# When the DeltaNet mixer's products come later in the written order

## The chip, the cores and the metric

The kernel runs as one program on one core of a Trainium2 chip. What is compared is the device time of one execution in microseconds (us), as the median of several runs.

## The reference

The reference is one step of a two-layer decoder trunk over 1,048 tokens: 8 samples that each add one token to an old state, 16 meta tokens and a prompt of 1,024. The first layer mixes tokens with a gated delta rule of 8 heads (128 wide), the second with latent attention; each is followed by a feed-forward layer with a short convolution. The change touches the first layer's mixer alone. Cut to that:

```
proj = h @ w_in                       # q, k, v (8 heads of 128 each), z, a, b
q, k, v = silu(causal convolution of width 4 over q, k, v)
q, k = l2norm(q), l2norm(k);  beta = sigmoid(b);  g = -exp(a_log) * softplus(a + dt_bias)
# prompt, in chunks, for each head; gc = cumulative sum of g inside the chunk
T = unit lower triangular matrix of (beta k k^T) * decay
u, w = solve(T, beta v), solve(T, beta k exp(gc))
for each chunk:                       # the recurrence
    v_new = u - w @ S
    o = (q exp(gc)) @ S + ((q k^T) * decay) @ v_new
    S = S * exp(gc_last) + (k exp(gc_last - gc))^T @ v_new
# samples: one step of the same rule from a state of their own
out = (rmsnorm(o) * silu(z)) @ w_out
```

The states S, the last rows before the convolution and the trunk's result are outputs.

## The kernel before

All matrices lie with channels on the partitions and tokens along the free dimension. TensorE's products with weights are made in three passes (`mm3`): weights and activations are each split into a high and a low part, and high x high, high x low and low x high are summed. The 1,048 tokens are cut into `CH`, pieces of 280, 384 and 384 columns.

The mixer is written as several streams (generators), one for each head and stage, and `merge` interleaves them: each stream yields a position before a piece of work, and the piece with the smallest position is written next. One unit is one head.

- `inproj(h)` runs from h to h + 1: the input projections (`psu`, 24 matmuls a piece) of q, k, v of head h and z of the head before. ScalarE copies a piece out of its bank (line 538, line 533 for the first piece); the projections have two banks (`mtile`).
- `chunks(h)` runs from h + 0.65 to h + 1.9, for 9 chunks of 116 tokens in three groups: transposes of k (`pstr`), the normalised `Kh` and its transposes (`pskt`, line 596), products `pskk` and the decay `E`; a store and reload of `U` in blocks of 32 (`ud`, `ins`); a substitution of 31 steps on VectorE (`tm`, `xs`, lines 658 and 660); a store and reload of the result (`xd`, `X`); products of blocks that complete the inverse (`psr`, line 680, `psx`, `psr2`, `psx2`), and u and w (`psu_`, `psw`), with GpSimd's `KG` and `KL`.
- `recur(h)` runs from h + 1.9 to h + 2.55: nine steps, in three groups. A step has `p1` = w S (line 754), a part of `pso`, `vn` on VectorE (line 757), `p2` (line 759), the rest of `pso` and the new `S` (line 765). After a group come the squares' sums and their scale `f`, the scaled output `on` (line 775), its turn by three transposes (`psot`, line 778), the product with the gate `z` (`og`, line 782) and the store to `og_d`. `on` and `og` take turns in one buffer (tag "on", one buffer). After the groups come the samples: `qkv8` normalised, `ps8t`, the product `p8`, a store of `vn` and its broadcast reload `vr`, the output `o8` and its turn (`pso8`, line 823), and the new states.
- `late_params` loads eight rows of the feed-forward convolution and turns them (`pfr`, line 488), in the buffers of tag "tm", which the substitution uses too.
- At the end `tail_a` and `tail_c` make the output projections of heads 0 to 5 (`psop`), `tail_b` turns the tokens once more (`pxr`, in `psA`); heads 6 and 7 follow.

Three pools hold the mixer's PSUM banks: `psA` has three (tag "g", the products of `chunks`), `psS` two for the recurrence's squares (`p1`, `p2`, `p8`), `psB` one, which `pso`, `psot`, `ps8t` and `pso8` share.

The written order is not yet the order on the engines: the framework that lowers the kernel offers instructions in the written order and places each on its engine when its inputs are there by its own model of the times. Then the order of each engine is fixed, and so is SP's, which issues nearly all transfers. On the chip an engine that comes to an instruction whose inputs are late waits.

Of the kernel before, what the change touches and what calls it, by code (L numbers as in the profile page):

```python
# [11 lines left out]
F32 = mybir.dt.float32  # L12
# [3 lines left out]
ALU = mybir.AluOpType  # L16
AX = mybir.AxisListType
PSUM = bass.MemoryType.PSUM
DRAM = bass.MemoryType.DRAM

P = 128
D = 1024
KT = D // P
NS = 8
# [37 lines left out]
def tile_step(ctx: ExitStack, tc: tile.TileContext, I, O, stop=None):  # L62
# [75 lines left out]
    def vc(nm, k=0):  # L138
        return vec[:, vcol[nm] + k:vcol[nm] + k + 1]
# [221 lines left out]
    psS = es.enter_context(tc.tile_pool(name="gsq", bufs=2, space=PSUM, reuse_waits="tile"))  # L361
    psB = es.enter_context(tc.tile_pool(name="gso", bufs=1, space=PSUM, reuse_waits="tile"))
# [34 lines left out]
    def gates():  # L397
# [65 lines left out]
        ps1 = psS.tile([P, NCK, H], F32, tag="s", name="psgl")  # L463
# [16 lines left out]
    def late_params():  # L480
        for l in range(2):
            for j in range(4):
                yield 2.0 + 0.08 * (4 * l + j)
                frow = rp.tile([2 * NFT, P], F32, tag="tm", name="frow")
                src = I["f_conv_w"][l, j] if j < 3 else I["f_conv_b"][l]
                SP.dma_start(frow, src.rearrange("(t p) -> t p", p=P))
                pt = psA.tile([P, 2 * NFT], F32, tag="g", name="pfr")
                PE.transpose(pt, frow, ident[:2 * NFT, :2 * NFT])
                V.tensor_copy(fcv[:, l, j, :], pt)
# [70 lines left out]
    def chunks(h, p0, p1):  # L560
# [12 lines left out]
        for g in range(3):  # L573
# [19 lines left out]
            yield pos(0.05 + 0.10 * g)  # L593
# [4 lines left out]
            yield pos(0.08 + 0.10 * g)  # L598
# [75 lines left out]
        for g in range(3):  # L674
            yield pos(0.73 + 0.02 * g)
            psr[g] = psA.tile([P, 3, 64], F32, tag="g", name="psr")
            R[g] = rp.tile([P, 3, 64], F32, tag="R", name="R", bufs=3)
            for i in range(3):
                k = 3 * g + i
                PE.matmul(psr[g][32:64, i, 0:32], U[0:32, k, 32:64], Tt[0:32, k, 0:32], start=True, stop=True)  # L680
                PE.matmul(psr[g][96:C, i, 0:32], U[64:96, k, 96:C], Tt[64:96, k, 0:32], start=True, stop=True)
            A.copy(R[g][32:64, :, 0:32], psr[g][32:64, :, 0:32])
            A.copy(R[g][96:C, :, 0:32], psr[g][96:C, :, 0:32])
        for g in range(3):
            gs = slice(3 * g, 3 * g + 3)
            yield pos(0.79 + 0.02 * g)
            psx = psA.tile([P, 3, 64], F32, tag="g", name="psx")
            for i in range(3):
                k = 3 * g + i
                PE.matmul(psx[0:32, i, 0:32], R[g][32:64, i, 0:32], X[32:64, k, 32:64], start=True, stop=True)  # L690
                PE.matmul(psx[64:96, i, 0:C - 96], R[g][96:C, i, 0:32], X[96:C, k, 96:C], start=True, stop=True)
                PE.matmul(psx[32:64, i, 32:64], X[32:64, k, 32:64], R[g][32:64, i, 0:32], start=True, stop=True)
            V.tensor_scalar(X[0:32, gs, 32:64], psx[0:32, :, 0:32], -1.0, None, op0=ALU.mult)
            V.tensor_scalar(X[64:96, gs, 96:C], psx[64:96, :, 0:C - 96], -1.0, None, op0=ALU.mult)
            V.tensor_scalar(Tt[32:64, gs, 0:32], psx[32:64, :, 32:64], -1.0, None, op0=ALU.mult)
# [7 lines left out]
        for g in range(3):  # L703
            yield pos(0.85 + 0.015 * g)
# [5 lines left out]
        for g in range(3):  # L710
            gs = slice(3 * g, 3 * g + 3)
            yield pos(0.9 + 0.015 * g)
# [6 lines left out]
        for g in range(3):  # L719
            gs = slice(3 * g, 3 * g + 3)  # L720
            yield pos(0.95 + 0.015 * g)
# [12 lines left out]
    def recur(h, p0, p1):  # L734
# [6 lines left out]
        S = None  # L741
        Ss = hp.tile([P, NS, P], F32, tag="Ss", name="Ss")
        SP.dma_start(Ss, I["state_delta_S"][0, :, h].rearrange("s k v -> k s v"))
        for g in range(3):
            gs = slice(3 * g, 3 * g + 3)
            pso = psB.tile([P, 3, P], F32, tag="o", name="pso")
            for i in range(3):
                yield pos(0.7 * (3 * g + i) / 9)
                k = 3 * g + i
                if S is None:  # L750
                    vn = uB[:, k, :]
                else:
                    p1_ = psS.tile([P, P], F32, tag="s", name="p1")
# [4 lines left out]
                p2 = psS.tile([P, P], F32, tag="s", name="p2")  # L758
# [17 lines left out]
            ps = psB.tile([P, 3 * C], F32, tag="o", name="psot")  # L776
            for i in range(3):
                PE.transpose(ps[:, C * i:C * i + C], on[:, i, :], ident[:C, :C])
            n = 3 * C if g < 2 else NP - 6 * C
            o0 = NS + 3 * C * g  # L780
            og = rp.tile([P, 3 * P], F32, tag="on", name="og", bufs=1)
            V.scalar_tensor_tensor(og[:, :n], ps[:, :n], vc("a_out"), hd["z"][:, o0:o0 + n], op0=ALU.mult, op1=ALU.mult)
            SP.dma_start(og_d[h][:, o0:o0 + n], og[:, :n])
# [11 lines left out]
        ps = psB.tile([P, 2, NS], F32, tag="o", name="ps8t")  # L795
# [4 lines left out]
        yield pos(0.78)  # L800
        p8 = psS.tile([P, P], F32, tag="s", name="p8")
# [9 lines left out]
        o8 = rp.tile([NS, P], F32, tag="vn", name="o8")  # L811
# [9 lines left out]
        yield pos(0.85)  # L821
        ps = psB.tile([P, NS], F32, tag="o", name="pso8")
        PE.transpose(ps, o8, ident[:NS, :NS])
        og8 = rp.tile([P, NS], F32, tag="og8", name="og8")
        V.scalar_tensor_tensor(og8, ps, vc("a_out"), hd["z"][:, 0:NS], op0=ALU.mult, op1=ALU.mult)
        SP.dma_start(og_d[h][:, 0:NS], og8)
# [5 lines left out]
        SP.dma_start(O["s_delta_S"][0, :, h].rearrange("s k v -> k s v"), Ss)  # L832

# [854 lines left out]
```

## Time and profile before

| | |
|---|---|
| median of 3 runs | 3309.26 us (3307.54 to 3319.37) |
| the profiled execution | 3314.68 us, its span 3312.9 us |
| mean granted TensorE clock | 0.975 |
| TensorE, matmuls | busy 94% of the span |
| VectorE, ScalarE, GpSimd | busy 61%, 38%, 26% |

The span runs from the first to the last instruction of the profiled execution; around it lie 1.8 us of that execution's time. The clock is given as a share of full speed. In the profile PE is TensorE's matmuls, PEld its weight loads, DVE VectorE, ACT ScalarE, POOL GpSimd, SPq the queue of SP; L778 is line 778 of the kernel, and `psot<-ident,on` says that `psot` is written from `ident` and `on`. The squares `p1`, `p2` and `p8` appear as `p`, and `pso8` as `pso`.

### The profile page before, as it was taken

Reading aid. Unit: us, or ns where it says so; the run is one execution under the profiler, and the core shown is the slowest. Engines: PE = TensorE matmul, PEld = TensorE weight load, DVE = VectorE, ACT = ScalarE, POOL = GpSimd, SP = SyncE. Lnnn points to the kernel's source line nnn. Section 1 sums busy time; section 2 is a strip of 40 time slices with the busy share of each in tenths; the row PEclk is TensorE's granted clock in tenths of the full one; section 3 lists DMA queues with packets and bytes.
Section 4 is the critical chain, followed back from the end, with each engine's and each line's share of the span. In section 5 each row is a group of like instructions: output and inputs, shape, how many; then the busy total and the mean of one; then the engine's idle time right before and its main releaser. Section 6 shows DMA issues by size and latency. Waiting matters only on the chain.

```text
span 3312.9 us, 52527 instructions
## 1 busy us (share of the span) xinstructions
PE 3123.5 (94%) x20846; PEld 2884.2 (87%) x20846; DVE 2030.3 (61%) x4139; ACT 1254.9 (38%) x2541; POOL 862.2 (26%) x1013
## 2 busy tenths in 40 slices
PE   7999999999899999999978999999998999999997
PEld 6888888888799999999967888856678999999996
DVE  4777777766864555555576676544557355555556
ACT  4656555563433222222334444433224322222223
POOL 1433222210342222322342111111105332322322
PEclk9999999999899999999989999999998999999999
DMA  3222222235321111111121000354432111111111
GB/s 107 62 65 69 64 67 59 72 105 176 96 66 46 39 52 49 48 46 39 45 86 44 25 27 28 108 189 184 159 102 84 46 46 45 46 45 52 46 39 66
DMA packets 267650, 235.08 MB, mean 71 GB/s; under 512 B 57919, under 2 KB 246597, under 8 KB 263285
## 3 DMA queue, kind: packets, MB, share of 16 engines
q1 hardware_dynamic: 260224, 189.69, 19.7%
q0 software_dynamic: 6912, 41.95, 3.4%
q8 instruction: 164, 2.69, 0.3%
q14 instruction: 82, 0.66, 0.1%
q10 hardware_dynamic: 268, 0.09, 0.0%
HBM read 198.84 MB, written 33.40 MB: 70 GB/s over the span
## 4 chain that ended last, share of the span: by engine, by line
PE 76%; DVE 14%; DMA 3%; issue 3%; ACT 2%; POOL 1%; SPq 0%; ACTq 0%; POOLq 0%; DVEq 0%
PE fps L228 9%; PE fps L229 9%; PE fps L227 9%; PE fdn L228 5%; PE fdn L227 5%; PE fdn L229 5%; PE psu L227 2%; PE psu L229 2%; PE po L1408 2%; PE psu L228 2%; PE dscr L1493 2%; DVE acc L287 2%; PE psop L227 1%; DVE tm L658 1%; DVE xs L660 1%
## 5 line engine op out<-in xcount | busy, mean ns | idle before, releaser
L144 POOL TENSOR_TENSOR ws<-ws,vec 128x1024 f32<-128x1024 f32 (+1 forms) x127 | 249.5, 1965 | 424.3 <-DMA ws<-in_f_w_up_dram 210.1
L228 PE MATMUL fps<-xfl,wh 128*128 128x384 f32 (+1 forms) x1056 | 343.7, 326 | 8.2 <-POOL xfl L295 8.1
L227 PE MATMUL fps<-xfh,wh 128*128 128x384 f32 (+1 forms) x1056 | 341.8, 324 | 8.0 <-ACT xfh L293 7.0
L228 PE MATMUL fps<-xbl,wh 128*128 128x384 f32 (+1 forms) x1056 | 343.6, 325 | 4.8 <-POOL xbl L295 4.7
L227 PE MATMUL fps<-xbh,wh 128*128 128x384 f32 (+1 forms) x1056 | 341.6, 324 | 1.1 <-ACT xbh L293 0.5
L229 PE MATMUL fps<-xfh,wl 128*128 128x384 f32 (+1 forms) x1056 | 342.4, 324 | 0.0
L229 PE MATMUL fps<-xbh,wl 128*128 128x384 f32 (+1 forms) x1056 | 341.2, 323 | 0.0
L966 DVE TENSOR_TENSOR fu<-fps,RS 128x384 f32<-128x384 f32 x176 | 98.0, 557 | 386.6 <-PE fps L229 386.1
L151 ACT CAST wh<-ws 128x1024 fp32r<-128x1024 f32 (+1 forms) x144 | 148.0, 1027 | 491.6 <-PE fps L228 373.8
L227 PE MATMUL fdn<-gh,dh 128*128 128x384 f32 (+1 forms) x960 | 315.2, 328 | 0.0
L228 PE MATMUL fdn<-gl,dh 128*128 128x384 f32 (+1 forms) x960 | 311.6, 325 | 0.0
L229 PE MATMUL fdn<-gh,dl 128*128 128x384 f32 (+1 forms) x960 | 308.6, 321 | 0.0
L1044 DVE TENSOR_TENSOR acc<-acc,fdn 128x384 f32<-128x384 f32 (+1 forms) x432 | 216.7, 514 | 108.8 <-PE fdn L229 108.0
L227 PE MATMUL psu<-xah,wh 128*128 128x384 f32 (+1 forms) x768 | 261.8, 341 | 9.5 <-ACT u L533 5.1
L228 PE MATMUL psu<-xal,wh 128*128 128x384 f32 (+1 forms) x768 | 260.0, 339 | 0.7 <-DVE xal L223 0.7
L229 PE MATMUL psu<-xah,wl 128*128 128x384 f32 (+1 forms) x768 | 259.0, 337 | 0.7 <-DVE wl L152 0.7
L975 DVE SCALAR_TENSOR_TENSOR fy<-fu,fcv,fy 128x1064 f32<-128x1064 f32 x176 | 238.6, 1357 | 7.6 <-ACT fy L973 7.3
L152 DVE TENSOR_TENSOR wl<-ws,wh 128x1024 fp32r<-128x1024 f32 (+1 forms) x144 | 173.6, 1206 | 71.3 <-ACT wh L151 71.1
L228 PEld LDWEIGHTS fps<-xfl,wh 128*128 128x128 f32 x1056 | 200.7, 190 | 10.8 <-POOL xfl L295 10.5
L227 PEld LDWEIGHTS fps<-xfh,wh 128*128 128x128 f32 x1056 | 200.3, 190 | 9.4 <-ACT xfh L293 7.9
L228 PEld LDWEIGHTS fps<-xbl,wh 128*128 128x128 f32 x1056 | 200.5, 190 | 6.9 <-POOL xbl L295 6.5
L227 PEld LDWEIGHTS fps<-xbh,wh 128*128 128x128 f32 x1056 | 200.2, 190 | 1.7 <-ACT xbh L293 0.9
(963 smaller groups left out, 7856.1 us busy)
## 6 DMA issues: line engine op xcount, KB each, us to landing
ws<-in_f_w_up_dram SPq DMA_DIRECT2D x88, 512.0 KB
ds<-in_f_w_down_dram SPq DMA_DIRECT2D x44, 512.0 KB
ws<-in_a_w_in_dram SPq DMA_DIRECT2D x32, 512.0 KB
xt<-in_x_prompt_dram SPq DMA_DIRECT2D x16, 512.0 KB
of<-og_d SPq DMA_DIRECT2D x32, 192.0 KB
xr<-x_d SPq DMA_DIRECT2D x16, 384.0 KB
GC<-gcd SPq DMA_DIRECT2D x24, 174.0 KB
Ss<-in_state_delta_S_dram SPq DMA_DIRECT2D x8, 512.0 KB
```

The lines of the kernel that those rows point to most:

```text
L144: G.tensor_tensor(st, st, bc(fo, [P, kt, m]), op=ALU.mult)
L151: A.copy(hi, st)
L152: V.tensor_tensor(lo, st, hi, op=ALU.subtract)
L227: PE.matmul(ps, wh, ah, start=start, stop=False)
L228: PE.matmul(ps, wh, al, start=False, stop=False)
L229: PE.matmul(ps, wl, ah, start=False, stop=stop)
L287: V.scalar_tensor_tensor(a_[:, k + j, :], a_[:, k + j, :], vc(wname, k + j), res[j], op0=ALU.mult, op1=ALU.add)
L966: V.tensor_tensor(u[:, 18 + t0:18 + t0 + n], ps[:, :n], RS[:, t0:t0 + n], op=ALU.mult)
L975: V.scalar_tensor_tensor(y, u[:, j:j + LW], fcv[:, l, j, tl:tl + 1], y, op0=ALU.mult, op1=ALU.add)
L1044: V.tensor_tensor(acc[c][:, m, :], acc[c][:, m, :], ps[:, :n], op=ALU.add)
L1408: PE.matmul(po[:, :nq], vt[:kk, kb, P * (h % 2):P * (h % 2) + P], pT[:kk, j, :nq], start=(kb == 0), stop=(kb == i))
L1493: PE.matmul(sc[32 * j:32 * j + 32, :], ql[:, k, b, :], cT[:, j, :], start=(k == 0), stop=False, tile_position=(0, 32 * j))
```

## The change

- The turn of a group's outputs (`psot`, `og`, the store) becomes `turn()`. It is called in the third step of the next group, for the last group at position 0.82 of `recur`, ahead of `p8`.
- The squares of the recurrence become four quarters of one tile in one bank (`sq4`); `pso` has two banks for itself, and `psot`, `ps8t`, `pso8` and the gates' `psgl` come from `psA`.
- The second half of a recurrence step has a position of its own, half a step later.
- `pskt` and `pskk` get positions 0.02 later; the block products begin later and follow each other more closely; the last part of `chunks` begins at 0.965 instead of 0.95.
- The samples' product `p8` goes from 0.78 to 0.82, the samples' turn from 0.85 to 1.25, behind the states; `o8` lies in another buffer for it.
- The rows of the feed-forward convolution come at distances of 0.16 instead of 0.08, and each is turned 0.1 after its load.

```diff
     psA = es.enter_context(tc.tile_pool(name="gps", bufs=3, space=PSUM, reuse_waits="tile"))
-    psS = es.enter_context(tc.tile_pool(name="gsq", bufs=2, space=PSUM, reuse_waits="tile"))
-    psB = es.enter_context(tc.tile_pool(name="gso", bufs=1, space=PSUM, reuse_waits="tile"))
+    psS = es.enter_context(tc.tile_pool(name="gsq", bufs=1, space=PSUM, reuse_waits="tile"))
+    psB = es.enter_context(tc.tile_pool(name="gso", bufs=2, space=PSUM, reuse_waits="tile"))
+    sq4 = psS.tile([P, 4, P], F32, name="sq4")
+    nsq = [0]
+
+    def square():
+        nsq[0] += 1
+        return sq4[:, nsq[0] % 4, :]
...
         V.tensor_copy(gc, ps1[:C])
-        ps1 = psS.tile([P, NCK, H], F32, tag="s", name="psgl")
+        ps1 = psA.tile([P, NCK, H], F32, tag="g", name="psgl")
...
             for j in range(4):
-                yield 2.0 + 0.08 * (4 * l + j)
+                yield 2.0 + 0.16 * (4 * l + j)
...
                 SP.dma_start(frow, src.rearrange("(t p) -> t p", p=P))
+                yield 2.1 + 0.16 * (4 * l + j)
...
             V.tensor_tensor(Kh[:, gs, :], ps[:C], bc(rk, [C, 3, P]), op=ALU.mult)
-            yield pos(0.05 + 0.10 * g)
+            yield pos(0.07 + 0.10 * g)
...
             A.copy(kt[:, 32 + 3 * C * g:32 + 3 * C * (g + 1)], ps.rearrange("p a b -> p (a b)"))
-            yield pos(0.08 + 0.10 * g)
+            yield pos(0.10 + 0.10 * g)
...
         for g in range(3):
-            yield pos(0.73 + 0.02 * g)
+            yield pos(0.795 + 0.012 * g)
...
             gs = slice(3 * g, 3 * g + 3)
-            yield pos(0.79 + 0.02 * g)
+            yield pos(0.84 + 0.012 * g)
...
         for g in range(3):
-            yield pos(0.85 + 0.015 * g)
+            yield pos(0.885 + 0.012 * g)
...
             gs = slice(3 * g, 3 * g + 3)
-            yield pos(0.9 + 0.015 * g)
+            yield pos(0.925 + 0.012 * g)
...
             gs = slice(3 * g, 3 * g + 3)
-            yield pos(0.95 + 0.015 * g)
+            yield pos(0.965 + 0.012 * g)
...
         S = None
+        done = []
+
+        def turn():
+            g, on = done.pop()
+            ps = psA.tile([P, 3 * C], F32, tag="g", name="psot")
+            for i in range(3):
+                PE.transpose(ps[:, C * i:C * i + C], on[:, i, :], ident[:C, :C])
+            n = 3 * C if g < 2 else NP - 6 * C
+            o0 = NS + 3 * C * g
+            og = rp.tile([P, 3 * P], F32, tag="on", name="og", bufs=1)
+            V.scalar_tensor_tensor(og[:, :n], ps[:, :n], vc("a_out"), hd["z"][:, o0:o0 + n], op0=ALU.mult, op1=ALU.mult)
+            SP.dma_start(og_d[h][:, o0:o0 + n], og[:, :n])
+
...
                 k = 3 * g + i
+                if i == 2 and done:
+                    turn()
...
                 else:
-                    p1_ = psS.tile([P, P], F32, tag="s", name="p1")
+                    p1_ = square()
...
                     V.scalar_tensor_tensor(vn, p1_[:C, :], nbt[:, k, h:h + 1], uB[:, k, :], op0=ALU.mult, op1=ALU.add)
-                p2 = psS.tile([P, P], F32, tag="s", name="p2")
+                yield pos(0.7 * (3 * g + i + 0.5) / 9)
+                p2 = square()
...
             V.tensor_tensor(on, pso[:C], bc(f, [C, 3, P]), op=ALU.mult)
-            ps = psB.tile([P, 3 * C], F32, tag="o", name="psot")
-            for i in range(3):
-                PE.transpose(ps[:, C * i:C * i + C], on[:, i, :], ident[:C, :C])
-            n = 3 * C if g < 2 else NP - 6 * C
-            o0 = NS + 3 * C * g
-            og = rp.tile([P, 3 * P], F32, tag="on", name="og", bufs=1)
-            V.scalar_tensor_tensor(og[:, :n], ps[:, :n], vc("a_out"), hd["z"][:, o0:o0 + n], op0=ALU.mult, op1=ALU.mult)
-            SP.dma_start(og_d[h][:, o0:o0 + n], og[:, :n])
+            done.append((g, on))
...
         yield pos(0.75)
-        ps = psB.tile([P, 2, NS], F32, tag="o", name="ps8t")
+        ps = psA.tile([P, 2, NS], F32, tag="g", name="ps8t")
...
         V.tensor_copy(kqz[:, 32:32 + 65 * 7 + 1:65], ps[:, 0, :])
-        yield pos(0.78)
-        p8 = psS.tile([P, P], F32, tag="s", name="p8")
+        yield pos(0.82)
+        turn()
+        p8 = square()
...
         SP.dma_start(vr, vd.rearrange("s v -> (s v)").partition_broadcast(P).rearrange("p (s v) -> p s v", s=NS))
-        o8 = rp.tile([NS, P], F32, tag="vn", name="o8")
+        o8 = sq[:, 1, :]
...
         V.tensor_scalar(o8, o8, qk, None, op0=ALU.mult)
-        yield pos(0.85)
-        ps = psB.tile([P, NS], F32, tag="o", name="pso8")
-        PE.transpose(ps, o8, ident[:NS, :NS])
-        og8 = rp.tile([P, NS], F32, tag="og8", name="og8")
-        V.scalar_tensor_tensor(og8, ps, vc("a_out"), hd["z"][:, 0:NS], op0=ALU.mult, op1=ALU.mult)
-        SP.dma_start(og_d[h][:, 0:NS], og8)
...
         SP.dma_start(O["s_delta_S"][0, :, h].rearrange("s k v -> k s v"), Ss)
+        yield pos(1.25)
+        ps = psA.tile([P, NS], F32, tag="g", name="pso8")
+        PE.transpose(ps, o8, ident[:NS, :NS])
+        og8 = rp.tile([P, NS], F32, tag="og8", name="og8")
+        V.scalar_tensor_tensor(og8, ps, vc("a_out"), hd["z"][:, 0:NS], op0=ALU.mult, op1=ALU.mult)
+        SP.dma_start(og_d[h][:, 0:NS], og8)
```

## Rows read from the trace of the kernel before

**Rows 1.** The page: busy time of each engine, share of the span, instructions.

```profile
PE 3123.5 (94%) x20846; PEld 2884.2 (87%) x20846; DVE 2030.3 (61%) x4139; ACT 1254.9 (38%) x2541; POOL 862.2 (26%) x1013
```

**Rows 2.** Busy time by stretch, the mixer; then clock, DMA share, GB/s.

```profile
core 0: us, PE busy (x) PEld busy (x) DVE busy (x) ACT busy (x) POOL busy (x), PEclk, DMA share, GB/s
50.00:850.00 800.00, 741.00 (x5609) 679.14 (x5610) 578.65 (x1692) 455.95 (x1243) 204.52 (x316) 0.97 0.31 83
```

**Rows 3.** TensorE's waits from 50 to 850 us: total, times, longest.

```profile
PE psot L778 <- DVE tm L658: 19.7, 4, 4.9
PE pxr L872 <- ACT xo L874: 6.0, 7, 2.3
PE psu L227 <- ACT u L533: 5.1, 5, 1.6
PE pskt L596 <- DVE Kh L592: 5.1, 5, 2.0
PE pso L823 <- DVE o L820: 4.8, 6, 1.1
PE psr L680 <- DVE Tt L668: 4.6, 3, 2.8
PE psot L778 <- DVE on L775: 3.8, 4, 2.3
PE pfr L488 <- DMA frow<-in_f_conv_w_dram: 1.6, 1, 1.6
...
PE p L754 <- DVE S L765: 1.1, 2, 0.9
PE pso L755 <- DVE og L782: 1.1, 1, 1.1
```

**Rows 4.** Timeline of TensorE: start, duration, instruction, idle time before it.

```profile
464.48 0.34 PE L229 MATMUL psu<-xah,wl 128*128 128x384 f32 x1
469.74 0.81 PE L778 MATMUL psot<-ident,on 116*128 116x116 f32 x3 [4.93 <-DVE tm L658]
...
557.49 0.81 PE L778 MATMUL psot<-ident,on 116*128 116x116 f32 x3 [4.94 <-DVE tm L658]
```

**Rows 5.** Stretches of 8 us around gaps; columns as in rows 2.

```profile
96.00:104.00 8.00, 6.02 (x30) 5.58 (x30) 7.79 (x12) 6.54 (x13) 6.64 (x10) 0.79 0.26 68
...
380.00:388.00 8.00, 5.66 (x28) 5.24 (x29) 7.68 (x23) 3.65 (x6) 1.94 (x3) 0.58 0.28 75
468.00:476.00 8.00, 6.26 (x28) 5.84 (x29) 7.15 (x21) 3.64 (x5) 1.33 (x3) 0.57 0.32 88
...
216.00:224.00 8.00, 5.80 (x33) 5.09 (x31) 7.83 (x27) 5.35 (x15) 4.02 (x7) 1.00 0.01 3
```

**Rows 6.** Timeline of VectorE and GpSimd ahead of the gap at 465.

```profile
460.18 1.98 DVE L581 TENSOR_SCALAR E<-GC,gc 116x116 f32<-116x116 f32 x1
...
462.21 0.27 DVE L581 TENSOR_SCALAR E<-GC,gc 116x116 f32<-116x116 f32 x1
...
460.15 1.93 POOL L144 TENSOR_TENSOR ws<-ws,vec 128x1024 f32<-128x1024 f32 x1
```

**Rows 7.** Timeline of ScalarE, the copy that frees a bank of `psu`.

```profile
468.62 0.47 ACT L538 COPY u<-psu 128x384 f32<-128x384 f32 x1
```

**Rows 8.** Timeline of TensorE, two matmuls of 280 columns in a row.

```profile
186.01 0.29 PE L227 MATMUL psu<-xah,wh 128*128 128x280 f32 x1
186.14 0.29 PE L228 MATMUL psu<-xal,wh 128*128 128x280 f32 x1
```

**Rows 9.** Timelines of VectorE and TensorE, the end of a recurrence step.

```profile
455.84 0.35 DVE L765 SCALAR_TENSOR_TENSOR S<-S,egl,p 128x128 f32<-128x128 f32 x1 [0.56 <-PE p L759]
...
456.24 0.37 PE L754 MATMUL p<-S,wT 128*116 128x128 f32 x1
```

**Rows 10.** Timeline of SP's queue; then VectorE's longest wait, 50 to 850 us.

```profile
812.27 0.30 SPq L808 DMA_DIRECT2D vd<-vn  x1
...
814.91 0.33 SPq L810 DMA_DIRECT2D vr<-vd  x1
...
DVE vr L830 <- DMA vr<-vd: 27.9, 7, 6.2
```

## The prediction

> **What bounds the kernel now.** I read the page first: TensorE is busy 94% of the span, and no other engine reaches two thirds [rows 1]. So time can come only out of TensorE's gaps, its clock, or its number of matmuls, and the change leaves that number as it is. Next I asked for the stretch that the change touches, the mixer. In the 800 us from 50 to 850 us TensorE is busy 741.0 us at a mean granted clock of 0.97; VectorE is busy 579 us of them, three quarters [rows 2]. TensorE therefore still sets the pace, and it has 59 us of gaps. The list of TensorE's waits in that stretch says where they are [rows 3]: one kind stands out, the turned outputs `psot`, which wait 19.7 us in only four places, 4.9 us each, for VectorE. The others are small and many.
>
> The timeline of one of the four shows the mechanism [rows 4]: the last matmul of `psu` starts at 464.48 and lasts 0.34 us, then nothing until `psot` at 469.74. It comes again 87.75 us later; that is the length of a head, by which I turn positions into time below (a position unit of `recur` is 0.65 heads or 57 us, of `chunks` 1.25 heads or 110 us). The cause stands on VectorE, which runs the next head's substitution (`tm`, `xs`) in the same stretch and is late: one `E` scaling took 1.98 us instead of 0.27, beside a GpSimd multiply of 1.93 us [rows 6].
>
> A gap costs more than its length. After the long ones the granted clock averages 0.57 or 0.58 over 8 us, after gaps of about 2 us 0.79; after one of 1.6 us it stays at 1.00 [rows 3, 5]. [...] Lost full-rate work, taken as (1 - clock) times TensorE's busy time: 0.42 x 5.66 = 2.4 us and 0.43 x 6.26 = 2.7 us in the two shown; the other two long ones look alike, so 10 us for four. At three shorter gaps (`pskt`, `psr`, one more `psot`) 0.21 x 6.0 = 1.3 us each, together 3.8 us.
>
> **The change part by part.** Times are those that TensorE gets back.
>
> Turned outputs, long waits. The three transposes of a group go from just behind `on` to the third step of the next group, two steps of 0.7/9 x 57 = 4.4 us, so 8.9 us later; the last group's go from position 0.622 to 0.82, 11 us later. Both exceed 4.94 us, so `on` will be there. What is late next? VectorE and ScalarE stay just as late, and TensorE goes on to the next `psu` product, c=0, 24 matmuls of 280 columns at 0.13 us [rows 8] = 3.1 us, from 464.82 to 467.9. The product behind it needs the bank that ScalarE's copy frees at 468.62 + 0.47 = 469.09 [rows 7]. So 1.2 us of each 4.93 stays: 4 x 3.7 = 14.9 us won, and the 10 us of clock with them, because 1.2 us is less than the gap that left the clock at 1.00.
>
> Turned outputs, the rest: 3.8 us waiting for `on` and 1.1 us of the next group's first product waiting for `og` [rows 3]. The second goes since `pso` has two banks and `psot` no longer shares its tag. With 1.3 us of clock that is 6.2; I take 5.
>
> Block products. `psr` moves from 0.73 to 0.795, 7.2 us later, against a longest wait of 2.8 us [rows 3]; the later products keep 4.4 to 5.0 us between one and the next (0.045 to 0.04 units instead of 0.06 to 0.05). 4.6 + 1.3 us of clock, all taken: 5.9. The GpSimd multiplies `KG` and `KL` go along, by 1.7 us or less. `pskt` moves by 0.02 units, 2.2 us, against a longest wait of 2.0: 5.1 + 1.3, I take 5.
>
> Samples. `pso8` goes from 0.85 to 1.25, 23 us later: its 4.8 us of waits [rows 3] go whole. Its store also leaves the place on SP ahead of the `xd` and `vr` transfers. The new place is 0.04 heads, 3.3 us, ahead of the next head's `z` copy into the same buffer; if VectorE were later than that, ScalarE's copy and so a `psu` bank would wait. I cost this at nothing with that cover.
>
> Convolution rows. The load is issued 0.1 heads, 8.8 us, ahead of its transpose instead of directly: 1.6 us won [rows 3]. The row holds one of two `tm` buffers meanwhile; the substitution that uses the other runs on VectorE alone and in order, so nothing is lost.
>
> Halves. The second half of a step is half a step, 2.2 us, later in order. TensorE waits little for `S` now, 1.1 us [rows 3]; I take 1. The squares `p1`, `p2`, `p8` now share a bank. That costs nothing, since a step is a chain by its data: `S` is read out from 455.84 to 456.19, and the next product starts at 456.24 [rows 9].
>
> Sum: 14.9 + 10 + 5 + 5.9 + 5 + 4.8 + 1.6 + 1 = 48 us.
>
> What it adds are waits that the trace does not have. First, `og` and `on` share one buffer, so a group's `on` must wait until the group before it has been stored; the store now starts one step (4.4 us) plus the squares and scales of the sums ahead of `on`, instead of three steps. VectorE would hold behind `on` the `S`, the copies of `u` and the substitution. Between issue and landing a small store takes up to 2.6 us (`vd` at 812.27, the transfer that needs it at 814.91); a large transfer keeps VectorE waiting up to 6.2 us [rows 10]. Second, five more pieces a head now draw on the three `psA` banks of the block products, and in the tail they share them with `pxr`, which already waits 6.0 us [rows 3]. Bounds: nothing, if the planner finds other work, and 16 waits of 2 to 3 us, 40 us, if none is covered. I take 11 us, nearer the first, because most of the waits of this stretch are about 1 us [rows 3]. Net: 48 - 11 = 37 us.
>
> The profiled execution took 3314.7 us by itself, 5.4 us above the median of the three runs, 3309.26. 3314.7 - 37 = 3277.7; less the same 5.4, the forecast is 3272 us.
>
> [...]
>
> **The rivals.** First, the lateness finds another reader. For it: ScalarE's copy that frees the bank came only at 468.62, four microseconds after the product ended at 464.82 [rows 4, 7], and VectorE's work is unchanged. Against it: one bank was free. If the four gaps shrink only to 2.4 us, the length at which the clock still falls, 4 x 2.5 = 10 us come back there instead of 25, and the net is 37 - 15 - 4 for further such waits = 18 us: 3291. Chance 0.18.
>
> Second, on the other side: the single `on`/`og` buffer. It decides as soon as the store lands over some 7 us after its transposes (a step of 4.4 us and about 3 us for squares and scales), for instance because SP holds it behind another transfer that waits. Then VectorE stands at `on` in two groups of each head, 16 times; at 3 us each that reaches TensorE as 48 us, and at the short gaps' 1.3 us of clock as 21 more: 69 - 48 = 21 us slower, about 3330. For it: SP takes transfers in order, and VectorE already waits 27.9 us in seven places for a transfer [rows 10]. Against it: the steps come some 3 us apart at their closest and sums add to it. Chance 0.07.
>
> Third, no gain at all: positions are only the order in which instructions are offered, and the framework's planner, with its own durations, may place the pieces where they were. Against it: the pieces would then have to be the only work on hand, but matmuls of `psu` are at hand. 3309, chance 0.07.
>
> Fourth, better: no new waits, and the gaps close whole. 48 us and the 4 x 1.2 left in the sum: 53 us, 3256. Chance 0.1.
>
> **How the numbers follow.** The forecast has 0.58, with a range of its own from 3258 to 3286 (new waits between 0 and 25 us). The range for 8 in 10 runs from 3250, below the fourth rival, to 3303: it takes in the first, and leaves out most of the second and third. A change of 0.5%, 16.5 us, is about what measurement can tell here, so faster means below 3292.7. The forecast gives 0.57 of its chance to that, the first rival 0.09 of 0.18, the fourth 0.1: 0.76. Slower is the second rival, 0.07. The rest, 0.17, is the same.
>
> **What would show it.** In the changed kernel's list of TensorE waits `psot` should have less than 5 us in all, `psr` and `pso8` less than 1 us each, and the 8 us stretches with a clock below 0.7 should be gone, one a head, so that heads follow each other in about 83 us instead of 87.75. Between 50 us and the end of the mixer TensorE's gaps should total 25 us or less instead of 59. The first rival would show as waits of `psu` for ScalarE's `u` of over 2 us where `psot` waited; the second as VectorE waiting at `on` for a transfer. I am wrong if `psot` still waits, if the clock still falls once a head, or if the gap's length reappears under `psu` or the recurrence.

## The result, and the profile after

The changed kernel takes 3346.96 us (median of four runs, 3343.61 to 3352.3), the kernel before, measured beside it, 3308.4 us. The ratio is 1.0113, with a 95% interval from 1.0085 to 1.0140: slower by 1.1% (the ratio is one of mean times; the medians differ by 38.6 us), where I had forecast 37 us faster. The time lies outside the range of 3250 to 3303 us.

The page's line of engines (busy time, share of the span, instructions) is that of [rows 1]; the same work takes longer:

```profile
PE 3123.1 (93%) x20846; PEld 2884.4 (86%) x20846; DVE 2043.3 (61%) x4139; ACT 1255.2 (38%) x2541; POOL 878.0 (26%) x1013
```

The loss lies in the mixer. Busy time by stretch, with the columns of [rows 2]:

```profile
50.00:850.00 800.00, 717.00 (x5435) 656.90 (x5436) 566.58 (x1641) 443.31 (x1221) 215.87 (x313) 0.95 0.29 76
```

TensorE's gaps in these 800 us are 83 us instead of 59, and the clock has fallen from 0.97 to 0.95. TensorE's waits from 50 to 880 us (total, times, longest) say where:

```profile
PE psr L687 <- DVE Tt L675: 39.2, 7, 8.3
PE pskt L603 <- DVE Kh L599: 7.3, 6, 2.0
...
PE sq L776 <- DVE S L788: 4.9, 6, 1.3
PE sq L782 <- DVE vn L779: 4.9, 11, 1.0
PE psx L697 <- DVE Tt L702: 4.5, 6, 0.7
PE psot L755 <- DVE on L798: 3.7, 4, 0.9
...
PE psot L755 <- DVE tm L665: 0.5, 1, 0.5
```

Against [rows 3], the turned outputs are cured: 23.5 us of waits have become 4.2, and the samples' turn no longer waits. The waits for `on` itself are what they were, 3.7 us instead of 3.8; the long ones behind the substitution are gone. But `psr`, which waited 4.6 us in all, now waits 39.2, once in each of seven heads (in the first, 2.8 us, as before). TensorE's timeline shows one such place, at the end of a piece of `psu`:

```profile
513.44 0.34 PE L229 MATMUL psu<-xah,wl 128*128 128x384 f32 x1
518.49 0.52 PE L687 MATMUL psr<-Tt,U 32*32 32x32 f32 x6 [4.72 <-DVE Tt L675]
```

The gap is as long as that under `psot` was [rows 4]. What follows differs: after `psot` came whole pieces of `psu`, after `psr` come products of 32 columns and transposes. One head from `psr` to the next `psr` in both kernels, before first (columns of [rows 2]):

```profile
503.60:590.50 86.90, 80.02 (x625) 74.19 (x624) 64.38 (x198) 51.05 (x144) 25.02 (x40) 0.96 0.27 69
```

```profile
518.50:609.70 91.20, 81.33 (x625) 74.93 (x625) 66.24 (x197) 51.33 (x143) 27.75 (x41) 0.93 0.25 65
```

A head is 4.3 us longer. Gaps are length minus busy time: 6.9 before, 9.9 after. Work lost to the clock I take as half of the time in which TensorE was busy at the half clock, a granted clock of 0.50: an estimate of 3.3 and 4.4 us (at 524 us of the changed kernel, at 0.50, matmuls of `psu` of 384 columns start 0.32 us apart, at 513 us, at 1.00, 0.17). Both together are 4.1 of the 4.3 us. (The product of the two means, (1 - clock) times busy time, gives 5.7 in the changed kernel; it is too much, because 2.6 us of the half clock lie in the gap ahead of the next `psr`.) The heads are not alike. From the first head's `psr` to the eighth's it takes 625.1 us instead of 591.4, which is more than the 28.9 us by which the two profiled executions differ: the first of these seven stretches is 6.5 us shorter than before, the second 12.0 longer, the next four 3.9 to 6.1, the last 9.2.

The chain behind the wait, on VectorE's and SP's timelines of the changed kernel, from the head's last `U` to `psr`:

```profile
461.02 0.83 DVE L611 SCALAR_TENSOR_TENSOR U<-pskk,bt,E 116x116 f32<-116x116 f32 x3 [0.39 <-PE pskk L608]
...
467.85 1.14 SPq L619 DMA_DIRECT2D ins<-ud  x3
...
510.41 0.18 DVE L667 TENSOR_TENSOR xs<-xs,tm 108x11 f32<-108x11 f32 x1
510.82 1.43 SPq L670 DMA_DIRECT2D xd<-xs  x3
...
515.99 1.73 SPq L673 DMA_DIRECT2D X<-xd  x4
...
517.98 0.46 DVE L675 STREAM_TRANSPOSE Tt<-X 32x288 f32<-32x288 f32 x1
```

From the end of `U` (461.85) to the end of the substitution (510.59) it takes 48.7 us, of which some 35 are the substitution, and 7.9 more to `psr`: the store, the reload, and the turn `Tt` on VectorE. In the substitution VectorE is the bound: its busy time, the third behind the stretch's length, is 98% of it:

```profile
475.00:510.60 35.60, 32.85 (x216) 31.17 (x215) 34.92 (x115) 22.43 (x48) 17.09 (x26) 1.00 0.15 43
```

So there are two lengths to compare: this chain, and the TensorE work that stands in order between `pskk`, which makes `U`, and `psr`, which ends the chain. I counted that work in the lowered programs, each instruction with the duration that its kind has in the trace: an estimate of 53.3 us in the kernel before and 50.1 in the changed one. The traces bear it out: in the fifth head TensorE's busy time between the last `pskk` and `psr`, half-clock time taken at full rate, is 52.4 and 49.7 us. One block of `psu` has gone from ahead of `psr` to behind it: 249 matmuls of `psu` were recorded there before, 221 after, and a block has 24.

### The profile page after: what moved, and what is told of

Its sections match the earlier page's. It is cut to its first block, busy times and chain, and to the rows that moved or that the text cites. A ratio compares the mean times of both kernels' runs of the same rounds, so it can differ in the third digit from the quotient of the medians.

```text
span 3341.8 us, 52471 instructions
## 1 busy us (share of the span) xinstructions
PE 3123.1 (93%) x20846; PEld 2884.4 (86%) x20846; DVE 2043.3 (61%) x4139; ACT 1255.2 (38%) x2541; POOL 878.0 (26%) x1013
## 4 chain that ended last, share of the span: by engine, by line
PE 73%; DVE 16%; DMA 3%; ACT 3%; issue 3%; POOL 1%; SPq 0%; ACTq 0%; DVEq 0%; POOLq 0%
PE fps L228 9%; PE fps L229 9%; PE fps L227 9%; PE fdn L228 5%; PE fdn L227 5%; PE fdn L229 4%; PE po L1425 2%; PE dscr L1510 2%; DVE tm L665 2%; DVE acc L287 2%; PE psop L227 1%; PE psu L227 1%; DVE xs L667 1%; PE psop L229 1%; PE psop L228 1%
## 5 line engine op out<-in xcount | busy, mean ns | idle before, releaser
L228 PEld LDWEIGHTS fps<-xfl,wh 128*128 128x128 f32 x1056 | 200.8, 190 | 10.4 <-POOL xfl L295 10.1
```

The lines of the kernel that those rows point to most:

```text
L228: PE.matmul(ps, wh, al, start=False, stop=False)
```

## The experiments

Theory one: the chain through VectorE has a fixed length, TensorE has too little work in order under it, and whichever reader of VectorE's work comes first inherits the lateness; the change took 3.2 us of work away from under it. Rivals: the new positions of the products of blocks cost the time (theory two), or the samples' turn by itself (theory three). All ratios are to the kernel before, measured beside each run; it took 3308 to 3321 us there, so the ratios can be compared and the medians cannot. Where I set a run against a forecast in us, I take its ratio times 3309.

| run | median us | ratio, 95% interval | work ahead of `psr`, us (estimate) |
|---|---|---|---|
| changed kernel | 3346.96 | 1.0113 (1.0085 to 1.0140) | 50.1 |
| e1 block and `pskt` positions back | 3380.59 | 1.0191 (1.0167 to 1.0214) | 50.0 |
| e2 samples' turn back | 3306.28 | 0.9976 (0.9964 to 0.9987) | 53.3 |
| e3 without weight scaling | 3315.15 | 0.9993 (0.9980 to 1.0006) | 50.1 |
| e4 idle products | 3370.13 | 1.0161 (1.0136 to 1.0186) | 52.9 |
| e5 blocks later | 3320.35 | 1.0023 (1.0003 to 1.0043) | 52.8 |
| e6 blocks latest | 3302.79 | 0.9968 (0.9946 to 0.9989) | 54.4 |
| e7 before, samples' turn alone | 3389.94 | 1.0214 (1.0171 to 1.0256) | 48.7 |
| e8 before, turned outputs alone | 3313.52 | 0.9988 (0.9972 to 1.0003) | 49.2 |
| e9 decay on ScalarE | 3344.85 | 1.0072 (1.0047 to 1.0097) | 50.1 |
| e10 e6 and decay on ScalarE | 3300.33 | 0.9942 (0.9917 to 0.9967) | 54.2 |
| e11 before, block and `pskt` positions alone | 3304.96 | 0.9965 (0.9946 to 0.9985) | 49 to 54 |
| e12 samples' turn in another bank | 3299.35 | 0.9957 (0.9940 to 0.9975) | 53.3 |

The last column does not order the times by itself: it says what stands under the chain, not which reader of VectorE's work comes first (e8), nor what the gap costs (e1). In the fifth head of each trace TensorE's work there, read as above, is 0.3 to 1.2 us below the estimate; for e6 and e10 the traces don't give it, because the next head's `pskk` comes ahead of `psr`.

What orders the runs better is whether the samples' turn starts ahead of `psr` or behind it (third to sixth heads of each trace). It starts 3 to 8 us behind `psr` in the changed kernel, e1, e3, e4, e7 and e9, with ratios from 1.0072 to 1.0214, and 0.9993 in e3, whose chain is shorter. It starts 8 to 27 us ahead in the kernel before and in e2, e5, e6, e8, e10, e11 and e12, with ratios from 0.9942 to 1.0023. The place of the turn and the work ahead of `psr` change together in most runs, so theory one and theory three in this form are not wholly parted; e3, in which the turn stays behind `psr`, speaks for the chain.

**e1: positions of the blocks and `pskt` back.** The five block positions and the two of `pskt` and `pskk`, as

```diff
-            yield pos(0.795 + 0.012 * g)
+            yield pos(0.73 + 0.02 * g)
```

> The changed kernel with two parts undone: pskt, pskk and the products of blocks are back at their old positions. Theory one (the chain through the substitution is as long as before, 56 to 61 us from U to psr, VectorE being busy in nearly all of it, and TensorE's ordered work under it too short; positions of pieces behind the chain change nothing in it): no change, 3347 us within 8, psr still waits 30 to 45 us in seven places. Theory two (the new positions of these parts put psr where it waits): back to about 3310 us, psr below 10 us of waits in all.

Theory two falls: undoing its positions makes the kernel slower still, 3372 us. Theory one had the wait right (`psr` 37.6 us in seven places) but not the time. The reason is the clock. The gap in the fifth head is 4.54 us, as in the changed kernel (4.72), but the stretches of 8 us behind it differ. The changed kernel, then this run:

```profile
520.00:528.00 8.00, 7.25 (x94) 6.41 (x89) 4.03 (x15) 5.30 (x25) 0.00 (x0) 0.50 0.38 112
528.00:536.00 8.00, 8.00 (x72) 6.57 (x71) 2.79 (x8) 3.54 (x14) 0.09 (x1) 0.96 0.01 2
```

```profile
541.00:549.00 8.00, 7.88 (x95) 5.97 (x90) 2.93 (x11) 5.63 (x22) 0.00 (x0) 0.50 0.34 95
549.00:557.00 8.00, 8.00 (x42) 7.01 (x41) 2.68 (x10) 3.19 (x14) 0.00 (x0) 0.50 0.01 2
557.00:565.00 8.00, 8.00 (x53) 7.90 (x53) 2.97 (x7) 1.79 (x4) 2.50 (x3) 0.78 0.00 0
```

With the blocks at the old positions all their products, and transposes, follow the gap with few matmuls of `psu` among them; TensorE is busy for 7.88 to 8.00 us of each 8 and stays at a granted clock of 0.50 until about 560. With the new ones `psu` comes in from 523.7, and the clock is back at 528.6. This head lasts 95.7 us with 9.3 of gaps, but 10.4 us lost to the clock instead of 4.4:

```profile
539.10:634.80 95.70, 86.43 (x625) 79.28 (x626) 66.02 (x197) 51.83 (x143) 27.92 (x41) 0.87 0.24 62
```

**e2: samples' turn back.** The six lines of the turn stand at 0.85 again, ahead of the states.

> The changed kernel with one part undone: the samples' turn is written at 0.85 again, ahead of the states. In the written program this puts psr 3.2 us later in TensorE's order behind the last pskk (53.3 instead of 50.1 us of work). Theory one (order under a chain of fixed length): the wait of psr falls from about 5 to about 2 us a head, 39 us in all to 15 to 20, and a wait of pso8 of up to 1 us a head returns; 7 x (3 + 1 of clock) less = about 3320 us. Theory two (the block products' positions): 3347. Theory three (the samples' turn is the whole cause): 3308, psr below 5 us.

This one part of the change turns its sign: 0.9976. `psr` waits 3.3 us in all. That is the outcome of theory three (3308 us, `psr` below 5 us), not of theory one, which left 15 to 20 us at `psr`. The lateness has moved to the samples' turn, the next reader, with more than the 1 us a head that I expected:

```profile
PE pso L840 <- DVE sq L837: 18.3, 6, 4.0
```

**e3: chain shortened by leaving work out.** `fold="a_pre"` is left out of the mixer's `wprep`.

> The changed kernel without GpSimd's multiplication of the mixer's input weights by a_pre (left out of the computation; TensorE, ScalarE, the transfers and the written order keep the rest). Three such multiplies of 1.92 us lie in each head's substitution. Theory one (VectorE's lateness in the substitution sets psr's time, and it is held up by GpSimd): the substitution of 35.3 us gets 3 to 5 us shorter, psr's wait falls from about 5 to 0 to 2 us a head, and the time to about 3315 us. Theory two (the positions): no change, 3347 us.

The direction is theory one's, and the gain is larger than its 3315 us: 3307. The substitution takes 32.3 us instead of 35.6, and a head 87.4 instead of 91.2. The written order is untouched, so the head follows the chain; the edit frees GpSimd and VectorE outside the substitution as well, and the two are not told apart (`pskt` and `S` wait less too, 2.6 us in all instead of 12.2). `psr` still waits 28.5 us in all, more than I expected: at 53.5 us from `U` to `psr` the chain is still longer than the work.

**e4: idle work ahead of `psr`.**

```diff
+            if g == 0:
+                fill = psA.tile([P, 352], F32, tag="g", name="fill")
+                for i in range(8):
+                    PE.matmul(fill[:108], ident[:108, :108], xs.rearrange("p a b -> p (a b)"), start=True, stop=True)
```

> The changed kernel with eight idle products more a head (116-row identity times xs, 352 columns, result read by nobody) just ahead of psr: about 4.8 us of TensorE work where it now waits 4.6 to 8.3 us. [...] If the clock after the gap costs nothing on the path: 3347 us, as the idle time is only filled. If TensorE's order is the bound and not the chain: 3385 us.

At 3362 us it is neither of these outcomes, nor is it the 3325 to 3332 us with which I had reckoned if half of the loss was the clock behind the gap. It doesn't settle the clock, since the products did not fill the gap: they wait for `xs` themselves, and `psr` comes 2 to 5 us after `Tt` is there. But it bears on the chain: in the fifth head it is 48.7 us from `U` to the end of the substitution, to the tenth the value of the changed kernel, though TensorE's order is another. The length is fixed only roughly: in the fourth to seventh heads of the two kernels and of all runs it is 45 to 50 us.

```profile
PE fill L686 <- DVE xs L667: 24.0, 6, 6.7
```

**e5 and e6: more work under the chain.** e5 offers the products of blocks at 0.85 to 0.98; e6 offers them at 0.88 to 0.98, stretches the chunks' stream from 1.25 to 1.32 heads (`CL`), and with it lets the recurrence begin 0.07 later and take 0.6 heads instead of 0.65 (`RL`):

```diff
-CL = 1.25
-RL = 0.65
+CL = 1.32
+RL = 0.6
...
-            yield pos(0.795 + 0.012 * g)
+            yield pos(0.88 + 0.006 * g)
...
-        yield pos(1.25)
+        yield pos(1.2)
```

> The changed kernel with the products of blocks offered later still (psr at 0.85 instead of 0.795, the others after it up to 0.98), the samples' turn left at 1.25. In the written program psr then has 52.8 us of TensorE work between it and the last pskk instead of 50.1. Theory one (the chain U to the end of the substitution is fixed at some 49 us, and what counts is how much of TensorE's order lies under it): as the run with the samples' turn back, 3300 to 3312 us, psr's wait 1 to 2.5 us a head and no half clock of 10 us. Theory three (the samples' turn's lateness itself, its store or its bank, costs the time): 3340 to 3350 us.

> The changed kernel with more still ahead of psr: the chunks' stream from h + 0.6 over 1.32 heads, the products of blocks at 0.88 to 0.98, the samples' turn at 1.2; 54.4 us of TensorE work between the last pskk and psr. Theory one: psr does not wait at all (54.4 us of order and some 2 to 4 us of small waits against 56.6 us of chain), no reader is left for the lateness, heads of 83 to 85 us, 3285 to 3300 us, faster than both. If the lateness finds yet another reader behind it (p8, pskt, psu): 3305 to 3320 us.

What I wrote ahead of e6 says that the stream begins at h + 0.6; its edit leaves the beginning at h + 0.65. So the gain of e6 is not that of the products of blocks alone. And in both runs the samples' turn, though offered late, comes 10 to 16 us ahead of `psr` again, so they don't try the work under the chain by itself.

e5 gains nine tenths of a per cent on the changed kernel with the samples' turn still offered late, but ends 0.2% above the kernel before, at 3317 us, between the two outcomes that I had named: `psr` still waits 15.4 us, `psot` for `on` 11.1. In e6 `psr` does not wait for more than 0.6 us, and the lateness is spread: `pskt` 14.5 us, `psot` 8.7, `p8` 7.1, the samples' turn 4.8. By its ratio, 3309 x 0.9968 = 3298 us, it ends at the slow end of theory one's range and beats both kernels; by its waits it is the other case, in which the lateness finds further readers.

**e7 and e8: two parts alone, in the kernel before.** e7 moves the samples' turn to 1.25, with its bank from `psA` and `o8` in `sq`; e8 has `turn()` and the new banks, and else only `o8` in its new buffer.

> The kernel before with one part of the change alone: the samples' turn at 1.25, in a bank of psA, o8 in the other buffer. In the written program psr moves from 53.3 to 48.7 us behind the last pskk, psot from 24.7 to 28.0. Theory one: psot's waits of 4.9 us shrink to 1 to 2 us, psr waits 5 to 7 us a head in their place, with small products behind it at the half clock: slower than before, 3330 to 3370 us. If the turned outputs are needed for the loss: 3305 to 3310 us.

> The kernel before with the turned outputs alone (turn() in the third step of the next group, four squares in one bank, two banks for pso); all positions of the products of blocks, pskt, halves, samples and rows as before, p8 at 0.78. In the written program psr lies 49.2 us behind the last pskk instead of 53.3. Theory one: psot's wait is won and psr inherits it, 5 us a head, with the products of blocks and transposes behind it at the half clock: 3340 to 3385 us. By my prediction's sum, 14.9 + 10 + 5 us for this part: 3280 us.

The samples' turn alone makes the kernel before 2.1% slower, more than the whole change does: `psr` waits 20.4 us, `psot` 18.2, and behind the wait the clock stays low for 20 to 31 us a head (summed over windows of 0.5 us), as in e1, where the blocks have their old positions too. Theory one's direction holds, its size was short of the clock, and it had the waits otherwise: 5 to 7 us a head at `psr`, which measured about 3, and 1 to 2 at `psot`, which measured 3.5 to 3.7.

The turned outputs alone change nothing. My sum had 30 us for them, and theory one 30 to 75 us of loss; both were wrong. The wait did pass on, but not to `psr`, although that stands early in order: it fell on the samples' product `p8` (the squares are called `sq` here), which starts at 468.1 in the head whose `psr` starts at 500.5. So 49.2 us of work ahead of `psr` did no harm here: the lateness had been waited for before.

```profile
PE sq L818 <- DVE kqz L813: 20.9, 5, 4.3
```

**e9 and e10: decay on ScalarE.** In the changed kernel, and in e6:

```diff
-                V.tensor_scalar(E[:, k, :], GC[:C, i, :], gc[:, k, h:h + 1], 0.0, op0=ALU.subtract, op1=ALU.min)
-            A.activation(E[:, gs, :], E[:, gs, :], AF.Exp)
+                A.activation(E[:, k, :], GC[:C, i, :], AF.Relu, scale=-1.0, bias=gc[:, k, h:h + 1])
+            A.activation(E[:, gs, :], E[:, gs, :], AF.Exp, scale=-1.0)
```

> The changed kernel with the nine differences of the decay E of a head on ScalarE (Relu of gc - GC, and the exponential of its negative: the same values) instead of VectorE, where they take 4.8 us of the 34.9 us that it is busy in the 35.6 us of the substitution. The written program keeps psr at 50.1 us of TensorE work behind the last pskk. Theory one (the chain through VectorE sets psr): the substitution falls from 35.3 to 31 to 32 us, psr's wait by 3 to 4 us a head, and the time to 3310 to 3325 us. If what sets psr is the transfers or TensorE's own order: 3340 to 3350 us.

> The kernel with the products of blocks latest (the sixth run here) and the decay's differences on ScalarE: more of TensorE's order under the chain (54.2 us) and a shorter chain. Theory one: both help, since the lateness that its readers divide among themselves (pskt 14.5 us, psot 8.7, p8 7.1, pso8 4.8 in that run) comes from VectorE: 3270 to 3292 us, faster than all the others. If TensorE's order alone was the bound there: 3300 us, as without it.

e9 missed: 4.8 us of VectorE's work left the stretch, and it got 1.3 us shorter. The groups of VectorE's instructions in the substitution (busy us, mean ns, idle before) of the changed kernel, then of e9, show why:

```profile
L667 DVE TENSOR_TENSOR xs<-xs,tm 108x84 f32<-108x84 f32 (+23 forms) x31 | 7.2, 234 | 0.3
L553 DVE SCALAR_TENSOR_TENSOR v<-u,acv,v 128x384 f32<-128x384 f32 (+1 forms) x9 | 5.9, 651 | 0.0
L588 DVE TENSOR_SCALAR E<-GC,gc 116x116 f32<-116x116 f32 x9 | 4.8, 533 | 0.0
```

```profile
L667 DVE TENSOR_TENSOR xs<-xs,tm 108x84 f32<-108x84 f32 (+23 forms) x31 | 9.5, 305 | 0.4
L553 DVE SCALAR_TENSOR_TENSOR v<-u,acv,v 128x384 f32<-128x384 f32 (+1 forms) x9 | 6.6, 731 | 0.0
```

The nine differences took 533 ns in the mean, against 270 ns for the one that came after GpSimd's multiply [rows 6]: two of them, at 0.91 and 1.98 us, ran beside GpSimd (its `KL` of 0.85 us and its multiply of the weights of 1.90 us) and make up the 2.4 us between. With them gone, `xs` and `v` take 2.3 and 0.7 us more; one `xs` of 1.82 us now stands beside GpSimd's multiply of the weights. So taking the differences out of VectorE left long instructions beside GpSimd's multiplies, while e3, which took the multiplies away, shortened the stretch from 35.6 to 32.3 us. Why VectorE's instructions last longer there, no run here shows.

The 1.3 us that were won did not reach `psr` either. The turn `Tt` stands on VectorE behind the samples' states (`vr`, `Ss`), and in e9 the next multiply of the weights, which in the changed kernel started at 517.86, beside `Tt`, came in among them:

```profile
509.00 2.19 DVE L841 TENSOR_SCALAR vr<-vr,kqz 128x128 f32<-128x128 f32 x2
...
509.19 1.92 POOL L144 TENSOR_TENSOR ws<-ws,vec 128x1024 f32<-128x1024 f32 x1 [7.53 <-DMA ws<-in_a_w_in_dram]
...
512.16 0.46 DVE L675 STREAM_TRANSPOSE Tt<-X 32x288 f32<-32x288 f32 x1
```

Two such `vr` take 0.48 us in the changed kernel. From `U` to `psr` it is 57.4 us in this head of e9, against 56.6. e10 is the fastest by its ratio, but does not stand apart from e6 (the intervals overlap).

**e11: positions of the blocks and `pskt` alone, in the kernel before.**

> The kernel before with the new positions of pskt, pskk and the products of blocks alone. By my prediction's sum, 5.9 + 5 us: 3298 us. By theory one: psr does not wait in the kernel before, so there is nothing to win behind it, 3300 to 3315 us; the 33 us that these positions are worth in the changed kernel (first run) are clock behind psr's wait, which is not there.

0.9965, some 11.6 us: the number of my prediction, 5.9 + 5 us for these two parts, but not by its way. `psr` waits 4.8 us, as before (4.6); `pskt` waits 2.1 instead of 5.1; and `psot` has three long waits of 4.3 to 4.9 us instead of four. From the first head's `psr` to the eighth's the profiled execution is 5.1 us shorter than that of the kernel before; where the rest comes from is open. Theory one, with nothing to win there, was wrong too.

**e12: one word.**

```diff
-        ps = psA.tile([P, NS], F32, tag="g", name="pso8")
+        ps = psB.tile([P, NS], F32, tag="o", name="pso8")
```

> The changed kernel with one word changed: the samples' turn, still offered at 1.25, takes its bank from the pool of pso instead of psA. In the written program it then stands some 100 rows ahead of psr on TensorE again instead of 24 rows behind it, and psr has 53.3 us of TensorE work behind the last pskk instead of 50.1. Theory one (what counts is the work under the chain; the samples' turn took it away because it draws on the three banks of the block products, not because it is late by its position): as the second run, 3300 to 3312 us, psr's waits below 5 us in all, 10 to 20 us of waits at the samples' turn. If its late position or its late store costs the time: 3340 to 3350 us.

The changed kernel with this word is faster than before: 0.9957. The samples' turn is offered at 1.25 as in the changed kernel, so the position by itself does not cost; e2, which keeps the bank and takes back the position, says the same of the bank. The loss needs both. In the changed kernel, with a bank from the pool of the block products, the turn was lowered behind `psr` (it starts 3.4 us after it), and `psr` a block of `psu` earlier; here it starts 16 us ahead of `psr`. Theory one had 3300 to 3312 us, under 5 us at `psr` and 10 to 20 at the samples' turn; it is 3295, 8.5 and 5.9. This head is 83.6 us long, with 4.6 us of gaps and 1.7 us lost to the clock:

```profile
PE psr L687 <- DVE Tt L675: 8.5, 3, 4.0
PE psu L227 <- ACT u L540: 6.9, 6, 1.7
PE pso L846 <- DVE sq L837: 5.9, 5, 2.3
```

```profile
494.00:577.60 83.60, 79.02 (x621) 72.76 (x622) 64.88 (x196) 50.13 (x143) 28.16 (x40) 0.98 0.28 72
```

## Why the prediction was wrong

**The turned outputs' long waits (14.9 + 10 us).** The step that failed first. I asked what TensorE's next instruction would wait for, found a bank of `psu`, and priced the rest of each gap at 1.2 us. I had written that VectorE stays just as late, but did not follow that lateness to the end of its chain. The chain ends at `psr`, some 57 us after `U`, while TensorE has 50 us of work for it; the difference is the 4.7 us at `psr` and smaller waits on the way. `psot` did stop waiting for the substitution, as I said; the 4.9 us came back at `psr` in the changed kernel and at `p8` in e8. Alone (e8) the part is worth 4 us at 0.9988, which is not clear of noise. Of the further 5 us for the rest of its waits, the 1.1 for `og` went and the 3.8 for `on` stayed (3.7).

**The samples (4.8 us won).** The step that made the sign. Its waits went, but the part costs 2.1% alone (e7), and with it undone (e2) or in another bank (e12) the change is faster than before. Against e12 it costs (1.0113 - 0.9957) x 3309 = 52 us, more than the whole loss. I had checked the buffer `z` and the queue of SP, and priced the draw on `psA` among the new waits, 11 us for all. What it did was no wait for a bank: it changed the lowered order, which I had taken to follow the positions: the turn starts 3.4 us behind `psr`, where it started 18 ahead. Why the planner then places `psr` a block earlier, no run here shows.

**The clock (2.4 to 2.7 us a long gap, carried over to every gap).** About right for a gap that `psu` follows, not as a price of a gap: with the same 4.5 to 4.7 us in front, 4.4 us a head were lost in the changed kernel and 10.4 in e1. So the new positions of the blocks and `pskt` are worth (1.0191 - 1.0113) x 3309 = 26 us there, as clock.

**Block products and `pskt` (5.9 + 5 us).** The size came out in e11, by luck: of the waits that were to go, `psr`'s stayed (4.8 us) and 3.0 of `pskt`'s 5.1 went. The longest wait of `psr`, 2.8 us in the first head, is there in the changed kernel too, with as many matmuls of `psu` ahead of it, 249, as before: its position had changed and its place in the order had not.

**The other parts.** `on` and `og` in one buffer, the second rival, did not show: `psot` waits 3.7 us for `on`, and VectorE nowhere waits at `on` for a transfer. The rows and halves were not tried alone. `pfr` still waits 2.9 us in two places where I had 1.6 us won. The recurrence's waits for `S` and `vn`, where I had 1 us won, grew from 1.6 to 9.8 us in the changed kernel, and to 3.5 in e12. And the forecast's own range has a slip: new waits between 0 and 25 us give 3261 to 3286, not 3258.

**The rivals.** The first, that the lateness finds another reader, was the mechanism. I sought it under `psu` and gave it a price of 15 us off the gain, because I let it shrink the gap. It kept the gap's full length or more (4.6 to 8.3 us), in six heads instead of four, and put it in front of work with which the half clock lasted 10 to 14 us instead of 6.8. The third rival was near the truth in its reason: the lowered order is not the order of positions.

Of what I had said would show the forecast right, e12 shows a part: from the second head's `psr` to the seventh's the heads are 83 to 85 us long, with no stretch of over 3.4 us at the half clock. The waits are not gone: `psr` has 8.5 us and `pso8` 5.9 where each was to have less than 1, `psot` 6.3 where it was to have less than 5, and from 50 to 850 us TensorE's gaps are 49 us, where they were to be 25. So it gives 14 us (0.9957 x 3309 = 3295), not 37. Of the 75 us between forecast and result, 52 are the samples' turn, and 23 are what e12 falls short of the forecast.

## What to carry to other kernels

When an engine waits for a chain that runs late on another, don't ask what it would do next; lay the chain's whole length beside the work that stands in order under it. Here the chain was longer, some 57 us against 50, and the wait that was moved came back at the next reader (39.2 us at `psr`, or 20.9 us at `p8` in e8); what paid was a shorter chain (e3), or an order that puts more work ahead of the reader that waits (e2, e12). A piece that is moved to another pool can change its place in the lowered order, and that of others with it (e12): read the lowered order before and after, not the positions. And look at what follows a gap: at gaps of 4.5 to 5.0 us the half clock lasted 6.8 us where `psu` followed (before) and 24 us where the products of blocks did (e1).

## What the runs showed of the hardware

The half clock at a gap lasted very different times. The granted clock was 0.50 for 6.8 us at each of the long gaps before (what of it lay in the gap included, as in the next two numbers), with `psu` following; for 10 to 14 us in the changed kernel; and for 24 to 27 us in six heads of e1, where TensorE was busy 96 to 97% of the time behind the gap, with products of 20 to 128 columns, transposes, and only 9 to 11 matmuls of `psu`. In e7 both stand in one run: gaps of 2.5 to 3.2 us at `psr` were followed by 20 to 24 us at the half clock in five heads, and gaps of 3.5 to 3.7 us at `psot`, with `psu` behind, by 3.4 us (6.8 in one). I had not expected a busy TensorE to stay at the lower clock. What in the work behind the gap decides it, the number, the width or the rows of the products, these runs do not tell apart.

Some of VectorE's instructions lasted longer beside GpSimd's multiplies of the weights. In the changed kernel a difference of 1.98 us, against 0.27 for the next one, stood beside a multiply of 1.90 us; in e9, without the differences, an `xs` of 1.82 us and a pair of `vr` of 2.19 us (beside 1.92 us) stood there in their place, where the other `xs` of that size took 0.25 us and a pair of `vr` in the changed kernel 0.48 us.
